# A chunked RWKV-7 scan: ScalarE copies the keys out of each score bank before VectorE masks it, and the stacked keys are copied later in the half-step

## The chip, the cores and the metric

The kernel runs on one core of one Trainium2 chip. The metric is the device time of one execution in microseconds. The core's engines run side by side, each through its own list of instructions in order: TensorE (PE in the profile; PEld is its weight load), VectorE (DVE), ScalarE (ACT), GpSimd (POOL, which here also issues DMAs) and SyncE (SP, which only issues DMAs). An instruction that needs another engine's result waits on a semaphore, and everything behind it on its own engine waits with it.

## The reference, cut to what matters

The model is a trunk of two layers over 1024 latent and 256 context tokens, width 1024, all in float32. Layer 0 mixes by pooling and neighbourhood attention, layer 1 by a bidirectional RWKV-7 recurrence, and each layer ends in an MLP. The change touches the recurrence of layer 1 alone. For each of 16 heads (64 wide) and each of two directions it is

```python
def step(S, inp):
    w_t, k_t, v_t, kk_t, kka_t = inp[:5]
    S = (S * w_t[:, :, None, :]
         - jnp.einsum('bhij,bhj->bhi', S, kk_t)[..., None] * kka_t[:, :, None, :]
         + v_t[..., None] * k_t[:, :, None, :])
    y = jnp.einsum('bhij,bhj->bhi', S, inp[5]) if emit else None
    return S, y
...
for d, reverse in enumerate((False, True)):
    decay_c, k_dc, a_c = dirs_c[d]
    s_ctx, y_c = wkv_scan(s0, decay_c, k_dc, v_c, kk_c, a_c, r_c, reverse)
    decay, k_d, a = dirs[d]
    _, y_d = wkv_scan(s_ctx, decay, k_d, v, kk, a, r, reverse)
    ys.append(y_d)
```

The context tokens come first and give the state from which the latent tokens start; only the latent tokens emit an output.

## The kernel before, in words

The scan (`l1_scan`, called once, after the features of layer 1) runs in chunks of 64 tokens: 20 steps `s`, of which 0 to 3 are context and 4 to 19 latent (`w["lat"]`). A step holds two half-steps, one for each direction `d`. All instructions of the loop stand in the order in which the code is written (a manual schedule); nothing reorders them.

In a half-step (s, d), three kinds of work are woven together.

- **The chain** of (s, d): `chain_x` multiplies the scores `ZQ[..., 1]` with the stacked state and values `D` into PSUM (`xp`), and ScalarE copies that to `XS` (L1679). `chain_u` multiplies by the chunk's inverse `TT` (`up`), and ScalarE writes the negative into `D` (L1688). `readout_state` (`yp`, L1701) and `readout_values` (`yp`, L1713) make the output, which ScalarE copies to `yt` (L1717) and SyncE stores. `chain_s` (`sp`, L1729) makes the new state, which VectorE adds and decays in two instructions (`SS`, L1734 and L1738). `carry`, called in the next half-step right behind `chain_x`, copies that state into the next step's `D` (two instructions, L1748) and then calls `stack`, which copies a part of the features `FT` into the upper half of the next step's `ZQ` (two instructions, L1608).
- **The scores** of the next step (n = s + 1, d): four groups `g`, two head pairs each. PE writes a group into the two PSUM banks of a tile `sc`, of which there are three. From these banks VectorE masks the scores into `ZQ` (L1632 for latent, L1639 for context steps) and ScalarE copies the token-major keys into `TM` (L1644).
- **The background**: `fill()`, called eight times in a half-step, takes the next pieces of the triangular inversions (`scan_invert`: two VectorE instructions each, L1511 and L1515), and from step 13 on pieces of the readout (`readout_sums`, L1966 to L1986, with long VectorE and GpSimd instructions over 128x1024) and splits of output weights.

For d = 1, `compose1` and `compose2` also run: two small products for the next inverse, with ScalarE's copies `G` (L1658) and `TT` (L1671). The pool `chps` gives the chain's products two PSUM buffers in turn, so a product waits until ScalarE or VectorE has emptied the one before the last.

A mask and a key copy of one group read the same two banks, and the program orders them by a semaphore: the key copy, second in the code, waits for the mask.

Of the kernel before, what the change touches and what calls it, by code (L numbers as in the profile page):

```python
# [58 lines left out]
class Trunk:  # L59
# [1466 lines left out]
    def l1_scan(self):  # L1526
        nc, a = self.nc, self.a
        with ExitStack() as es:
# [35 lines left out]
            def load(s, d, parts=range(4)):  # L1564

                if s >= NSTEP:
                    return
                w = W[s]
                F = w["F"][d] = FTs[(2 * s + d) % 4]
                f0 = 0 if w["lat"] else 1  # L1570
                for i in parts:
                    w["got"].add((d, i))
                    hs = slice(2 * i, 2 * i + 2)
                    (nc.scalar if s == 0 else nc.gpsimd).dma_start(out=F[:, hs, 1 + f0:], in_=self.ft[s, d, :, hs, f0:])

            def load_values(s, d):
                D_ = hp_.tile([128, 8, 2, CH], F32, tag=f"D{d}", name="D")
                (nc.gpsimd if s == 0 else nc.sync).dma_start(
                    out=D_[64:128], in_=rows_of(self.v1scr, s, d).rearrange("t (h e i) -> t h e i", e=2, i=CH)
                )  # L1580
                W[s]["D"][d] = D_
# [15 lines left out]
            def load_inverses(s, e):  # L1597
                if s >= NSTEP:
                    return
                TT = W[s]["TT"] = TTs[s % 2]  # L1600
                for bl in range(2):
                    r = slice(e * 64 + bl * 32, e * 64 + bl * 32 + 32)
                    nc.sync.dma_start(out=dh(TT[r, :, :, bl * 32:bl * 32 + 32]), in_=quarter(lt_[s // 2], s, bl, e))

            def stack(s, d):

                for e in range(2):
                    nc.scalar.copy(out=W[s]["ZQ"][d][0:64, :, e, 1], in_=W[s]["F"][d][st[e], :, 2])  # L1608

            def scores(s, d, g):  # L1610


                w = W[s]
                F = w["F"][d]
                more = s + 1 < NSTEP
                if g == 0:
                    w["ZQ"][d] = zp.tile([128, 8, 2, 2, CH], F32, tag="ZQ", name="ZQ")
                    if more:
                        w["TM"][d] = zp.tile([128, 8, 128], F32, tag="TM", name="TM")
                assert (d, g) in w["got"]  # L1620
                ps = scps.tile([128, 2, 512], F32, tag="sc", name="sc")
                p4 = ps[:, :, 0:384].rearrange("p e (j f t) -> p j e f t", j=2, f=3)
                f = slice(0, 3) if w["lat"] and more else slice(1, 3) if w["lat"] else slice(0, 3, 2)
                for j in range(2):
                    for e in range(2):
                        nc.tensor.matmul(
                            out=p4[:, j, e, f], lhsT=F[st[e], 2 * g + j, 3:5].rearrange("p a t -> p (a t)"), rhs=F[st[e], 2 * g + j, f],
                            start=True, stop=True,
                        )
                hs = slice(2 * g, 2 * g + 2)  # L1630
                if w["lat"]:
                    nc.vector.tensor_tensor(  # L1632
                        out=w["ZQ"][d][:, hs].rearrange("p j e f t -> p j e (f t)"),
                        in0=ps[:, :, 0:384].rearrange("p e (j n) -> p j e n", j=2)[:, :, :, CH:],
                        in1=masks[:, d, 1:3].rearrange("p f t -> p (f t)").unsqueeze(1).unsqueeze(1).to_broadcast([128, 2, 2, 2 * CH]),
                        op=ALU.mult,
                    )
                else:
                    nc.vector.tensor_tensor(  # L1639
                        out=w["ZQ"][d][64:128, hs, :, 1], in0=p4[64:128, :, :, 2],  # L1640
                        in1=masks[64:128, d, 2:3].unsqueeze(1).to_broadcast([64, 2, 2, CH]), op=ALU.mult,
                    )
                if more:
                    nc.scalar.copy(out=w["TM"][d][:, hs].rearrange("p j (e i) -> p j e i", e=2), in_=p4[:, :, :, 0])  # L1644

            def compose1(s):

# [25 lines left out]
            def chain_x(s, d):  # L1673
                w = W[s]
                xp = chps.tile([128, 8, CH], F32, tag="ch", name="xp")
                for h in range(8):
                    for e in range(2):
                        nc.tensor.matmul(out=xp[st[e], h], lhsT=w["ZQ"][d][:, h, e, 1], rhs=w["D"][d][:, h, e], start=True, stop=True)
                nc.scalar.copy(out=XSs[d], in_=xp)  # L1679
# [63 lines left out]
            def carry():  # L1743

                while late:
                    s, d = late.pop()
                    for e in range(2):
                        nc.scalar.copy(out=W[s]["D"][d][0:64, :, e], in_=SS[d][st[e]])  # L1748
                    stack(s, d)

            def background():

                blocks = self.scan_blocks(ip, NCC // 2, nc.sync.dma_start)
                for b in range(NCC // 2, NSTEP // 2):
                    yield
                    for i, _ in enumerate(self.scan_invert(ip, b, *blocks)):
                        if i == 16 and b + 1 < NSTEP // 2:
                            blocks = self.scan_blocks(ip, b + 1, nc.sync.dma_start)
                        yield
                pace[0] = 1  # L1760
                self.readout_weight_load(8)
                self.readout_weight_load(0)
                for _ in range(6):
                    yield
                self.readout_weight(8)
                yield
                self.readout_weight(0)
                yield
                self.readout_gate_load(READ_ORDER[0])
                yield from self.readout_all(READ_ORDER[:4], lambda t: step[0] >= EARLY[t])  # L1770
                self.readout_gate(READ_ORDER[0])
                self.readout_gate_load(READ_ORDER[1])
                for k in (1, 2, 3):
                    self.readout_weight_load(k)
                for _ in range(4):
                    yield
                self.readout_weight(1)
                self.readout_weight_load(4)

            bg, late = background(), []  # L1780

            pace, step, turn = [2.1], [0], [0]

            def fill():
                turn[0] += pace[0] / 2
                while turn[0] >= 1:
                    turn[0] -= 1
                    next(bg, None)
# [23 lines left out]
            for s in range(NSTEP - 1):  # L1812
                n = s + 1
                step[0] = s
                if s == 2:
                    pace[0] = 2.45
                later = ((s + 1, 1), (s + 2, 0)) if s else ((NSTEP, 1), (s + 2, 0))
                for d in range(2):
                    load_values(n, d)
                    chain_x(s, d)  # L1820
                    carry()
                    scores(n, d, 0)
                    load(*later[d], (2,))
                    fill()
                    scores(n, d, 1)
                    fill()
                    chain_u(s, d)
                    load(*later[d], (3,))
                    fill()
                    if d:  # L1830
                        compose1(n)
                    else:
                        load_blocks(s + 2, 0)
                    scores(n, d, 2)
                    fill()
                    readout_state(s, d)
                    chain_s(s, d)
                    load(s + 2, d, (0,))
                    fill()
                    readout_values(s, d)  # L1840
                    if d:
                        load_inverses(s + 2, 0)
                    else:
                        load_blocks(s + 2, 1)
                    fill()
                    scores(n, d, 3)
                    load(s + 2, d, (1,))
                    fill()
                    if d:
                        compose2(n)  # L1850
                        load_inverses(s + 2, 1)
                    fill()
            for _ in bg:
                pass
            s = NSTEP - 1
            for d in range(2):
                chain_x(s, d)
                carry()
            self.readout_weight(2)
            self.readout_weight_load(5)  # L1860
            for d in range(2):
# [384 lines left out]
```

## Time and profile before

| what | value |
| --- | --- |
| median of 3 runs | 3560.07 us (3559.86 to 3560.34) |
| the profiled execution | 3557.76 us, span 3555.6 us |
| mean granted TensorE clock | 0.962 |
| busy share of the span: PE, PEld, DVE, ACT, POOL | 93%, 77%, 58%, 40%, 12% |
| first and last product of `xp` (the scan) | 2208.6 and 2673.2 us |
| start of `XS` of step 3 d = 0, step 4 d = 0, step 18 d = 0 | 2281.47, 2303.00, 2646.55 us |
| duration of mask L1632, key copy L1644, stack copy L1608 | 684, 368, 617 ns (means) |

All times in the profile count from the start of the span. "Idle before" is the time for which an engine stood still before an instruction, with the instruction that released it. An engine's busy share over the whole span says little about the scan; there, one reads for each engine what its waits were and who ended them.

### The profile page before, as it was taken

The numbers are of one execution on the slowest core, as the hardware profiler recorded it, in microseconds if no ns is written. First come the engines' busy times: TensorE is split into PE (matmuls) and PEld (weight loads), VectorE is DVE, ScalarE is ACT, GpSimd is POOL, SyncE is SP. The second block draws the span as 40 slices with busy tenths as digits, with TensorE's granted clock in tenths as the row PEclk, the third lists the DMA queues.
The fourth block names the chain that finished last, engine by engine and source line by source line (L and its number), as shares of the span: only waits on it lengthen the run. The fifth ranks groups of instructions, "written<-read, shape, count | busy, mean of one in ns | idle before, by whom it ended". The sixth has DMA issues, their size and how long they took to land. (4 is left out here: it accounts for less than half of the span.)

```text
span 3555.6 us, 62546 instructions
## 1 busy us (share of the span) xinstructions
PE 3295.9 (93%) x25466; PEld 2752.1 (77%) x25466; DVE 2052.2 (58%) x3903; ACT 1434.7 (40%) x2743; POOL 430.9 (12%) x564
## 2 busy tenths in 40 slices
PE   8999889999999999989988776888888899999998
PEld 4787767888888888868878775777776788888887
DVE  4255555344444444596658997888665734444446
ACT  4244446311121211276667664556654521111112
POOL 0010110010000000024420002223241200000000
PEclk9999989999999999999999997899989999999999
DMA  8432333222222211143227678788763411111112
GB/s 280 151 91 83 102 126 132 88 84 83 83 84 83 76 44 36 42 148 100 70 69 222 211 232 243 159 196 202 214 177 116 165 49 48 48 48 48 48 48 77
DMA packets 432623, 409.11 MB, mean 115 GB/s; under 512 B 151584, under 2 KB 362400, under 8 KB 432336
## 3 DMA queue, kind: packets, MB, share of 16 engines
q1 hardware_dynamic: 405376, 321.55, 30.5%
q0 software_dynamic: 24640, 81.81, 7.4%
q8 instruction: 200, 3.28, 0.4%
q10 hardware_dynamic: 2320, 1.77, 0.2%
q14 instruction: 87, 0.71, 0.1%
HBM read 292.54 MB, written 112.49 MB: 114 GB/s over the span
## 5 line engine op out<-in xcount | busy, mean ns | idle before, releaser
L916 DVE TENSOR_TENSOR yacc<-yps,yacc 128x512 f32<-128x512 f32 x540 | 369.6, 689 | 304.3 <-PE yps L93 303.9
L74 ACT CAST wh<-st 128x1024 fp32r<-128x1024 f32 x160 | 165.0, 1049 | 760.5 <-PE yps L93 557.8
L93 PE MATMUL yps<-wh,xh 128*128 128x512 f32 x1152 | 453.3, 393 | 3.7 <-DVE yacc L916 2.1
L93 PE MATMUL yps<-wh,xl 128*128 128x512 f32 x1152 | 448.6, 390 | 0.7 <-DVE xl L75 0.7
L93 PE MATMUL yps<-wl,xh 128*128 128x512 f32 x1152 | 449.0, 390 | 0.0
L75 DVE TENSOR_TENSOR wl<-st,wh 128x1024 fp32r<-128x1024 f32 x160 | 194.2, 1228 | 277.6 <-ACT wh L74 277.5
L93 PE MATMUL acc<-h2h,wh 128*128 128x426 f32 (+3 forms) x768 | 275.7, 359 | 3.0 <-ACT y L671 3.0
L93 PE MATMUL acc<-h2h,wl 128*128 128x426 f32 (+3 forms) x768 | 274.2, 357 | 0.0
L93 PE MATMUL acc<-h2l,wh 128*128 128x426 f32 (+3 forms) x768 | 274.0, 357 | 0.0
L93 PEld LDWEIGHTS yps<-wh,xh 128*128 128x128 f32 x1152 | 216.2, 188 | 71.7 <-DVE yacc L916 12.7
L93 PEld LDWEIGHTS yps<-wh,xl 128*128 128x128 f32 x1152 | 216.2, 188 | 47.8 <-DVE xl L75 2.3
L93 PEld LDWEIGHTS yps<-wl,xh 128*128 128x128 f32 x1152 | 216.3, 188 | 44.9 <-issue 1.7
L898 DVE TENSOR_TENSOR r<-r 128x428 f32<-128x428 f32 (+4 forms) x164 | 102.3, 624 | 242.4 <-ACT r L897 242.4
L93 PE MATMUL acc<-mh,wh 128*128 128x256 f32 (+1 forms) x640 | 216.4, 339 | 4.3 <-ACT mh L74 4.2
L93 PE MATMUL acc<-ml,wh 128*128 128x256 f32 (+1 forms) x640 | 215.7, 337 | 0.0
L93 PE MATMUL acc<-mh,wl 128*128 128x256 f32 (+1 forms) x640 | 215.3, 337 | 0.0
L93 PE MATMUL acc<-h2bh,wh 128*128 128x512 f32 (+3 forms) x544 | 211.4, 389 | 1.4 <-ACT wh L74 0.7
L93 PE MATMUL acc<-h2bl,wh 128*128 128x512 f32 (+3 forms) x544 | 211.2, 388 | 0.7 <-DVE h2bl L288 0.7
L93 PE MATMUL acc<-h2bh,wl 128*128 128x512 f32 (+3 forms) x544 | 210.9, 388 | 0.3 <-DVE wl L75 0.3
L897 ACT ACTIVATE r<-acc 128x428 f32<-128x428 f32 (+4 forms) x164 | 89.1, 543 | 293.8 <-PE acc L93 269.0
L93 PEld LDWEIGHTS acc<-h2h,wh 128*128 128x128 f32 x768 | 145.0, 189 | 16.1 <-issue 5.1
L74 ACT CAST xh<-r 128x428 fp32r<-128x428 f32 (+4 forms) x164 | 93.3, 569 | 148.0 <-DVE r L898 148.0
(322 smaller groups left out, 7057.5 us busy)
## 6 DMA issues: line engine op xcount, KB each, us to landing
st<-in_mlp_w SPq DMA_DIRECT2D x128, 512.0 KB
ft<-F SPq DMA_DIRECT2D x64, 512.0 KB
FT<-ft POOLq DMA_DIRECT2D x128, 256.0 KB, 5.6
adas<-in_ada_w POOLq DMA_DIRECT2D x112, 256.0 KB, 3.8
adas<-in_ada_w SPq DMA_DIRECT2D x80, 256.0 KB
x<-x SPq DMA_DIRECT2D x28, 512.0 KB
bias<-in_bias SPq DMA_DIRECT2D x64, 192.0 KB
ls<-ls SPq DMA_DIRECT2D x80, 128.0 KB
```

Of the source, the lines that this page charges most:

```text
L74: self.nc.scalar.copy(out=hi, in_=src)
L75: self.nc.vector.tensor_tensor(out=lo, in0=src, in1=hi.bitcast(F32), op=ALU.subtract)
L93: self.nc.tensor.matmul(out=ps, lhsT=lhs[x], rhs=rhs[y], start=first and i == 0, stop=last and i == 2)
L897: nc.scalar.activation(out=r, in_=ps, func=AF.Relu)
L898: nc.vector.tensor_tensor(out=r, in0=r, in1=r, op=ALU.mult)
L916: nc.vector.tensor_tensor(out=yacc[t][:, n], in0=ps, in1=yacc[t][:, n], op=ALU.add)
```

## The change

It moves two things in each engine's list and takes nothing away. In `scores` the key copy is written ahead of the mask, so that the mask now waits for the key copy. In `carry` the call of `stack` is replaced by a note in the list `stacks`, which the loop works off behind the third group of scores; in the last step it is worked off right behind `carry`, as before.

```diff
                 hs = slice(2 * g, 2 * g + 2)
+                if more:
+                    nc.scalar.copy(out=w["TM"][d][:, hs].rearrange("p j (e i) -> p j e i", e=2), in_=p4[:, :, :, 0])
                 if w["lat"]:
                     nc.vector.tensor_tensor(
...
-                if more:
-                    nc.scalar.copy(out=w["TM"][d][:, hs].rearrange("p j (e i) -> p j e i", e=2), in_=p4[:, :, :, 0])
...
                     for e in range(2):
                         nc.scalar.copy(out=W[s]["D"][d][0:64, :, e], in_=SS[d][st[e]])
-                    stack(s, d)
+                    stacks.append((s, d))
...
-            bg, late = background(), []
+            bg, late, stacks = background(), [], []
...
                     scores(n, d, 2)
+                    while stacks:
+                        stack(*stacks.pop())
                     fill()
                     readout_state(s, d)
...
             for d in range(2):
                 chain_x(s, d)
                 carry()
+                while stacks:
+                    stack(*stacks.pop())
```

ScalarE in the half-step s = 8, d = 1, from the state's copy to the inverse's. Before, the stack copy (`ZQ`) stands between the state's copies (`D<-SS`) and the first key copies (`TM`), ahead of the chain's values (`D<-up`):

```order
L1679 COPY XS_19567<-xp 128x512
L1748 COPY D<-SS 64x8x64 x2
L1608 COPY ZQ<-FT_19564 64x8x64 x2
L1644 COPY TM<-sc 128x256 x2
L1688 ACTIVATE D<-up 64x8x64 x2
L1658 ACTIVATE G<-p_23001 32x512 x2
L1644 COPY TM<-sc 128x256
L1717 COPY yt<-yp 128x512
L1644 COPY TM<-sc 128x256
L1671 COPY TT_19569<-p_23125 32x16x32 x2
```

The same place now (line numbers are those of the changed file, in which the key copy is L1632):

```order
L1679 COPY XS_19567<-xp 128x512
L1748 COPY D<-SS 64x8x64 x2
L1632 COPY TM<-sc 128x256 x2
L1688 ACTIVATE D<-up 64x8x64 x2
L1658 ACTIVATE G<-p_22999 32x512 x2
L1632 COPY TM<-sc 128x256
L1608 COPY ZQ<-FT_19564 64x8x64 x2
L1717 COPY yt<-yp 128x512
L1632 COPY TM<-sc 128x256
L1671 COPY TT_19569<-p_23125 32x16x32 x2
```

The two stack copies moved behind the third key copy, just ahead of `yt`; no other instruction of ScalarE changed its place.

VectorE around the last mask ahead of the state update of the same half-step, with the semaphores that each row waits for (PE, DVE itself, Activation for ScalarE). Before:

```order
L1632 TENSOR_TENSOR ZQ<-sc,masks 128x512 [waits PE_49]
L1511 TENSOR_TENSOR tmp<-X,M 128x135 [waits DVE_49]
L1515 TENSOR_TENSOR X<-X,tmp 128x5x27 [waits DVE_49]
L1734 TENSOR_TENSOR SS<-sp,SS 128x512 [waits PE_49,Activation_49]
L1738 TENSOR_TENSOR SS<-SS,pcs 128x512 [waits DVE_49]
```

And now:

```order
L1634 TENSOR_TENSOR ZQ<-sc,masks 128x512 [waits Activation_49]
L1511 TENSOR_TENSOR tmp<-X,M 128x135 [waits DVE_49]
L1515 TENSOR_TENSOR X<-X,tmp 128x5x27 [waits DVE_49]
L1734 TENSOR_TENSOR SS<-sp,SS 128x512 [waits PE_49]
L1738 TENSOR_TENSOR SS<-SS,pcs 128x512 [waits DVE_49]
```

VectorE's order is the same; the mask waits for ScalarE instead of PE, and the key copies of ScalarE, which waited for VectorE before, now wait for PE alone. The lists of PE, POOL and SP keep their order; `chain_x`'s first products of `xp` now also wait for the stack copy, which is later.

## The prediction

> **What bounds the scan now.** I cut the scan into three stretches by the starts of `XS` and read busy time and granted clock in each. Columns: PE, PEld, VectorE, ScalarE and GpSimd busy, granted clock, DMA share, GB/s. The first row is context steps 1 to 3, the second steps 4 to 12 (full scores with inversions), the third steps 13 to 18 (inversions over, output weights and readout beside the scan).
>
> ```profile
> 2236.73:2303.00 66.27, 52.78 (x1168) 46.42 (x1164) 57.11 (x148) 39.01 (x78) 19.42 (x26) 0.87 0.74 163
> 2303.00:2516.17 213.17, 182.41 (x4608) 161.42 (x4608) 184.23 (x455) 127.89 (x253) 65.03 (x92) 0.97 0.81 196
> 2516.17:2668.46 152.29, 128.75 (x3060) 114.54 (x3056) 96.18 (x124) 92.15 (x173) 59.51 (x54) 0.89 0.72 197
> ```
>
> No engine is full. ScalarE works 60% of the time (127.89 of 213.17). So I asked who waits for whom, over the whole scan (us in total, times, longest):
>
> ```profile
> ACT TM L1644 <- DVE ZQ L1632: 86.2, 49, 6.1
> DVE SS L1734 <- PE sp L1729: 44.1, 30, 4.2
> ACT TM L1644 <- DVE ZQ L1639: 34.9, 13, 6.8
> PE sp L1729 <- ACT D L1688: 29.3, 24, 6.4
> PE yp L1701 <- ACT D L1688: 18.8, 14, 2.7
> PE up L1686 <- ACT XS L1679: 18.2, 19, 4.3
> ```
>
> A ring: ScalarE's key copy waits for a mask (86.2 + 34.9 = 121.1 us); behind it stand `XS` and the chain's values, for which PE waits (66.3 us); VectorE then waits for PE's `sp` (44.1 us). Masks stand behind inversions and readout on VectorE, so VectorE's backlog reaches PE through ScalarE.
>
> One half-step in order of time (step 8, d = 1), ScalarE first, then PE, then VectorE; the brackets hold the idle time before:
>
> ```profile
> 2409.24 0.37 ACT L1644 COPY TM<-sc 128x256 f32<-128x256 f32 x1 [1.56 <-DVE ZQ L1632]
> 2409.51 0.59 ACT L1679 COPY XS<-xp 128x512 f32<-128x512 f32 x1
> 2410.13 1.26 ACT L1748 COPY D<-SS 64x512 f32<-64x512 f32 x2
> 2411.41 1.25 ACT L1608 COPY ZQ<-FT 64x512 f32<-64x512 f32 x2
> 2412.57 0.63 ACT L1644 COPY TM<-sc 128x256 f32<-128x256 f32 x2
> 2413.09 1.21 ACT L1688 ACTIVATE D<-up 64x512 f32<-64x512 f32 x2
> 2414.33 1.19 ACT L1658 ACTIVATE G<-p 32x512 f32<-32x512 f32 x2
> 2415.54 0.37 ACT L1644 COPY TM<-sc 128x256 f32<-128x256 f32 x1
> 2417.70 0.58 ACT L1717 COPY yt<-yp 128x512 f32<-128x512 f32 x1 [1.79 <-PE yp L1713]
> ```
>
> ```profile
> 2408.91 1.57 PE L1626 MATMUL sc<-FT 64*128 64x192 f32 x16
> 2410.42 1.15 PE L1686 MATMUL up<-XS,TT 64*64 64x64 f32 x32
> 2411.49 1.20 PE L1653 MATMUL p<-ZT,G 32*32 32x32 f32 x64
> 2412.62 0.92 PE L1626 MATMUL sc<-FT 64*128 64x192 f32 x8
> 2414.36 1.15 PE L1701 MATMUL yp<-SS,FT 64*64 64x64 f32 x32 [0.81 <-ACT D L1688]
> 2415.57 1.15 PE L1729 MATMUL sp<-D,TM 128*64 128x64 f32 x32
> ```
>
> ```profile
> 2410.90 0.68 DVE L1632 TENSOR_TENSOR ZQ<-sc,masks 128x512 f32<-128x512 f32 x1
> 2413.59 0.69 DVE L1632 TENSOR_TENSOR ZQ<-sc,masks 128x512 f32<-128x512 f32 x1
> 2416.84 0.69 DVE L1734 TENSOR_TENSOR SS<-sp,SS 128x512 f32<-128x512 f32 x1 [2.01 <-PE sp L1729]
> ```
>
> `XS` is late because of the key copy; the values (2413.09) are late because 1.25 us of stack copies stand ahead of them; `yp` needs a PSUM buffer that the values empty, and waits 0.81.
>
> **The stack copies.** Moved, not removed: 74 of the 80 leave the place ahead of the values (the first step's four and two of the last stay). In the half-step above, `XS` would start right behind `xp` (about 2409.0), state copies end at 2410.9, two key copies at 2411.5, and the values wait for `up`, which ends at 2411.55: they run to 2412.8 instead of 2414.3. PE is through with `sc` at 2413.5 and starts `yp` there, not at 2414.36. In the new place the copies end at 2412.8 + 1.19 (`G`) + 0.37 + 1.25 = 2415.6. Next is `yt`, and the 1.79 us that ScalarE idled before it are the cover: `yp` would be complete at about 2416.7. If a readout piece filled that gap, `yt` would be late by up to 1.25, and with it the PSUM buffer. The copies also wait for the fourth mask of the half-step before; PE's third score group needs that mask's banks too (three tiles), so the wait is already over. `xp`, the reader, comes after 2418: nothing. No DMA moves; GpSimd's loads into `FT` a step later see the stack copy done, and SyncE's store of `yt` keeps its place.
>
> **The swapped pair.** ScalarE's copy then waits for PE only; the 121.1 us go, and what ScalarE gains lies idle unless PE gets `XS` and the values earlier. VectorE's mask pays: it starts no sooner than the key copy's end. The first mask, 2410.90 before, would wait to about 2411.2; the third needs its key copy, behind `G`, and moves from 2413.59 to about 2414.35. `SS` stands one mask and an inversion piece further on, at about 2415.85; `sp` ends at about 2415.7. So `SS` starts 1.0 us earlier than 2416.84, and VectorE, no longer PE, sets it. Next late are the state copy behind `SS` and PE's scores waiting for a mask's banks.
>
> **Steps 4 to 12.** The cap is what VectorE waits now, because its 455 instructions stay:
>
> ```profile
> DVE SS L1734 <- PE sp L1729: 18.0, 16, 3.1
> DVE ZQ L1632 <- PE sc L1626: 1.6, 3, 1.1
> ```
>
> 19.6 us; the half-step worked out gives 1.0, and eighteen of them 18. Where inversion pieces are short, PE sets the pace and some waiting stays; I take 14. Ends: 4, if the masks' new waits eat most of it, and 19.6.
>
> **Steps 0 to 3.** The same question from 2218 on, behind a wait for a DMA that stays:
>
> ```profile
> DVE SS L1734 <- PE sp L1729: 3.6, 3, 1.7
> DVE ZQ L1639 <- PE sc L1626: 1.8, 3, 1.4
> DVE SS L1738 <- PE sp L1729: 1.6, 2, 1.4
> ```
>
> 7.0 us at most; I take 4, near the share of the stretch above (14 of 19.6 would be 5), less a little because context scores are short and the key copies stand closer to the masks. Ends: -1 and 7.
>
> **Steps 13 to 18.** VectorE has room (96.18 of 152.29), but long readout instructions stand ahead of masks. Step 15, d = 1 (ScalarE, PE, VectorE):
>
> ```profile
> 2581.93 0.37 ACT L1644 COPY TM<-sc 128x256 f32<-128x256 f32 x1 [2.41 <-DVE ZQ L1632]
> 2582.20 1.21 ACT L1688 ACTIVATE D<-up 64x512 f32<-64x512 f32 x2
> ```
>
> ```profile
> 2579.83 0.92 PE L1626 MATMUL sc<-FT 64*128 64x192 f32 x8
> 2583.46 1.98 PE L1701 MATMUL yp<-SS,FT 64*64 64x64 f32 x32 [2.71 <-ACT D L1688]
> ```
>
> ```profile
> 2583.46 0.68 DVE L1632 TENSOR_TENSOR ZQ<-sc,masks 128x512 f32<-128x512 f32 x1
> 2587.38 0.69 DVE L1734 TENSOR_TENSOR SS<-sp,SS 128x512 f32<-128x512 f32 x1 [3.24 <-PE sp L1729]
> ```
>
> Here a key copy blocks the values until 2582.20. Free of it they follow `up` at about 2578.8 and end at 2580.0; `yp` then starts behind `sc`, at 2580.7, and `sp` ends near 2583. `SS` would come right behind the mask that ends at 2584.14: 3.2 us earlier. Such a half-step comes once in each of three readout steps: 3 x 3.2 = 9.6. The other nine I price at 0.9 each, a little under the 1.0 above: 8.1. Together 17.7, taken as 18. Ends: 8, if GpSimd and VectorE's long instructions are what counts, and 37, all PE idle time (152.29 - 128.75 = 23.5) with the clock it lost (11% of 128.75 = 14).
>
> Sum: 4 + 14 + 18 = 36 us off the profiled execution's 3557.76, which lies 2.3 below the median of the runs: 3560.07 - 36 = 3524. All lowest ends together give 11 us, all highest 64.
>
> Part of that 14 rests on the clock. Behind an idle time of 0.81 us `yp` took 1.15 us; behind 2.71 us it took 1.98. [...]
>
> **Rivals.**
>
> The wait changes sides but not its size: VectorE, with 184.23 of 213.17 us busy the fullest beside PE, stands at masks behind ScalarE's queue, and little comes back at `SS`. For it: a mask's copy is now third or fourth in a queue that holds the state copies (1.26) and `G` (1.19). Against it: in the half-step above the masks move by 0.3 and 0.76 and `SS` has 2.01 to give. Price: 4 for steps 4 to 12, 8 to 11 later, 1 in context: about 15 us off, 3545.
>
> Slower: the first mask of each half-step waits behind `XS` and the state copies (0.59 + 1.26 + 0.37 = 2.2 us from the end of `xp`), while its scores are there after 0.8. That is up to 1.4 us each in the 26 half-steps of steps 0 to 12: 36 us, against 26.6 us of VectorE waiting (19.6 + 7.0) that can absorb it. It decides from about 1.0 us a half-step on. With 1.4 everywhere and nothing gained later: +10 us, 3570. Against it: VectorE is usually late at the first mask, as at 2410.90. [...]
>
> No change: PE's waits for ScalarE give way to waits for `FT` loads or stored inverses. The DMA share is 0.81 in steps 4 to 12 and would rise to 0.81 x 213 / 199 = 0.87; no wait of PE for a load stands among the large ones above. Price: 0, 3560.
>
> Much more: all the idle time of PE closes, 50 us or more off, 3507.
>
> **How the numbers follow.** Forecast case 0.70 (3508 to 3536 by itself, two thirds of the way to its ends), much more 0.08, changed sides 0.14, no change 0.04, slower 0.04. A range of 3502 to 3547 holds the forecast case, most of the much-more case and most of the changed-sides case. 0.2% of 3560 is 7 us, about what this measurement can tell from no change: faster 0.92, same 0.04, slower 0.04.
>
> **What would show it.** Right: key copies no longer wait for masks; `XS` and the values stop being what PE waits for; in steps 4 to 12 VectorE's waits for `sp` are under 6 us and the stretch takes about 199 us; steps 13 to 18 take about 134; `D<-SS` waits for `SS` here and there. Wrong: large new rows in which masks wait for key copies, or `xp` for the stack copy, or `yt` late with PE waiting for it; or GpSimd's loads arriving behind the scores that need them.

## The result, and the profile after

The changed kernel takes 3536.67 us (median of four runs, 3529.58 to 3543.92); before took 3559.97 (four runs, 3554.97 to 3560.34). The ratio is 0.9938, 95% interval 0.9915 to 0.996: faster by 23 us, where 36 were forecast (3524, range 3502 to 3547). The profiled execution of after is the fastest, 3529.58 us, 28.2 under the profiled one of before.

The waits over the whole scan of after (us in total, times, longest; the key copy is now L1632, the mask L1634, in context steps L1641):

```profile
DVE ZQ L1634 <- ACT TM L1632: 43.7, 29, 6.2
DVE ZQ L1641 <- ACT TM L1632: 15.2, 8, 6.3
ACT XS L1679 <- PE xp L1678: 32.4, 26, 4.8
ACT TM L1632 <- PE sc L1626: 20.1, 42, 1.8
DVE SS L1734 <- PE sp L1729: 8.5, 11, 1.6
ACT D L1748 <- DVE SS L1738: 9.3, 4, 5.0
PE xp L1678 <- issue: 7.7, 4, 4.0
PE p L1667 <- issue: 7.6, 6, 2.4
```

The ring is open: no key copy waits for a mask (121.1 us before), VectorE's wait for `sp` fell from 44.1 to 8.5 us, and PE's waits for `XS` and the values (66.3 us) are gone from the head of the list. PE's waits for the stack copy ahead of `xp` did not grow (2.7 us, 2.6 before). Two things stand in their place: masks wait for key copies (58.9 us), and PE waits for "issue", that is for nothing the profile names.

The three stretches of after (same columns as before's three rows):

```profile
2230.83:2291.55 60.72, 50.50 (x1154) 44.63 (x1153) 55.91 (x144) 39.74 (x79) 19.34 (x26) 0.86 0.82 171
2291.55:2502.42 210.87, 185.38 (x4610) 164.60 (x4612) 186.00 (x462) 131.16 (x253) 66.08 (x93) 0.95 0.84 202
2502.42:2639.13 136.71, 124.54 (x3072) 110.97 (x3070) 94.32 (x127) 93.18 (x173) 58.32 (x54) 0.93 0.78 219
```

Against 66.27, 213.17 and 152.29: steps 1 to 3 lost 5.5 us (with step 0, which went from 26.76 to 23.39, it is 8.9), steps 13 to 18 lost 15.6, and the longest stretch, steps 4 to 12, only 2.3. (Another 2.5 us lie ahead of the first `XS`.) So the question is where the gain of steps 4 to 12 went.

The half-step worked out in the prediction (step 8, d = 1) came as worked out. PE, then VectorE:

```profile
2398.69 1.57 PE L1626 MATMUL sc<-FT 64*128 64x192 f32 x16
2403.25 1.15 PE L1701 MATMUL yp<-SS,FT 64*64 64x64 f32 x32
2404.33 1.15 PE L1729 MATMUL sp<-D,TM 128*64 128x64 f32 x32
```

```profile
2404.33 0.69 DVE L1634 TENSOR_TENSOR ZQ<-sc,masks 128x512 f32<-128x512 f32 x1 [0.51 <-ACT TM L1632]
2405.53 0.69 DVE L1734 TENSOR_TENSOR SS<-sp,SS 128x512 f32<-128x512 f32 x1
```

From the start of `sc` to `SS` it is 6.84 us, before 7.93: 1.09 earlier, where 1.0 was forecast. `yp` has no wait (0.81 before), the third mask pays 0.51.

Other half-steps of the stretch look different. PE's order of time in step 7 of after:

```profile
2375.83 1.02 PE L1701 MATMUL yp<-SS,FT 64*64 64x64 f32 x26
2379.70 0.39 PE L1701 MATMUL yp<-SS,FT 64*64 64x64 f32 x6 [2.84 <-issue]
...
2386.22 0.63 PE L1667 MATMUL p<-TT,G 32*32 32x32 f32 x15 [2.36 <-issue]
2386.78 1.98 PE L1678 MATMUL xp<-D,ZQ 128*64 128x64 f32 x32
2388.68 2.93 PE L1626 MATMUL sc<-FT 64*128 64x192 f32 x16
```

A run of 32 matmuls that needs nothing further stops for 2.84 us after the 26th; 127 matmuls later it happens again, and behind that pause `xp` takes 1.98 us instead of 1.15 and `sc` 2.93 instead of 1.57. Counted along PE's queue, such pauses of the stretch lie 127, 253, 378 to 379, 504 to 506 or 757 matmuls apart: multiples of about 126 (the expectations below write 128). The DMA queues of the stretch say why that number (packets, MB, share of 16 engines):

```profile
q8 instruction: 37, 0.61, 1.4%
```

37 packets for 4610 matmuls and 4612 weight loads are about 250 instructions each: PE's own instructions come by DMA, some 126 matmuls a packet. The trace has the time of every packet, and it shows that the pauses are blocks that come late: at each of the 13 pauses on these multiples (over 0.3 us) PE goes on 1.28 to 1.68 us after a packet of q8 has landed, and over all the kernels below, at 123 such pauses, 1.2 to 2.0 us after. The packet that ends the pause of 2.84 us, for one, starts to move at 2376.78 and lands at 2378.02. The pauses add up to 15.8 us in steps 4 to 12 of after, and to 2.3 us in before. Two more waits for "issue" in after, 1.81 and 1.63 us ahead of `xp`, lie off the multiples and follow no packet in this way; they are not counted, nor are their like below.

### The profile page after: what moved, and what is told of

The parts are those of the page before. It is cut to its first block, busy times and chain, and to the rows that moved or that the text cites. A ratio compares the mean times of both kernels' runs of the same rounds, so it can differ in the third digit from the quotient of the medians.

```text
span 3527.5 us, 62517 instructions
## 1 busy us (share of the span) xinstructions
PE 3289.8 (93%) x25466; PEld 2747.2 (78%) x25466; DVE 2049.0 (58%) x3903; ACT 1440.4 (41%) x2743; POOL 430.9 (12%) x564
## 5 line engine op out<-in xcount | busy, mean ns | idle before, releaser
L1626 PE MATMUL sc<-FT 64*128 64x192 f32 (+1 forms) x1280 | 144.3, 357 | 16.6 <-issue 6.5
```

The source lines that it names most:

```text
L1626: nc.tensor.matmul(out=p4[:, j, e, f], lhsT=F[st[e], 2 * g + j, 3:5].rearrange("p a t -> p (a t)"), rhs=F[st[e], 2 * g + j, f], start=True ...
```

## The experiments

All ratios are to the kernel before, timed on the same chip.

**Each part alone, and the change again.** `swap_only` keeps the key copy first and puts the stack copies back:

```
 carry():  -  stacks.append((s, d))
           +  stack(s, d)
```

> The swapped pair alone; the stack copies stay behind the state copies. Both theories: most of the gain is here, 15 to 20 us off before (about 3542), since the 121 us in which key copies waited for masks go; in steps 4 to 12 the values are still late by the 1.25 us of stack copies, so PE waits there for values again, about 8 us. Theory A (VectorE's backlog sets steps 4 to 12): that stretch is 209 to 213 us, as with the whole change. Theory B (PE's instructions come late, in blocks of 128 matmuls, when DMA is busy): pauses in the middle of PE's runs are fewer than the 14 us of the whole change, since PE waits elsewhere meanwhile.

`stack_only` moves the stack copies and keeps the mask first:

```
-                if more:
-                    nc.scalar.copy(out=w["TM"]...)     # ahead of the masks
...
+                if more:
+                    nc.scalar.copy(out=w["TM"]...)     # behind them
```

> The stack copies moved, the mask still ahead of the key copy. Key copies still wait for masks (over 90 us in all). Values come up to 1.25 us earlier where no key copy holds them up: 3 to 8 us off before (about 3555). No change at all would mean that the move alone is worth nothing without the swap.

`after_again` has no edit.

> The changed kernel a second time, for its spread. Theory A: the waits follow from the order of the program, so steps 4 to 12 take 210 to 212 us again and the pauses at blocks of 128 matmuls do not move the time. Theory B: the pauses differ from one execution to the next (they hang on what DMA is doing at that moment), and the stretch and the whole time move with their sum, about 1 us for each us of pause; runs spread over 10 us or more, while before stays within 6.

The swap alone: 3549.12 us against 3557.15, ratio 0.9974 (0.9964 to 0.9983). The stack copies alone: 3546.12, ratio 0.9968 (0.9955 to 0.9981). Both: 3530.87, ratio 0.9922 (0.991 to 0.9934). So 8.0 and 11.0 us apart, 26.3 together: neither part carries the change. The 7 us above the sum of the two are just clear of the spread of these runs; against the 23 us of the first result they would be 4. I had expected 15 to 20 of the swap and 3 to 8 of the stack copies. Steps 4 to 12 of each, in that order (length, PE, PEld, VectorE, ScalarE, GpSimd, clock, DMA share, GB/s):

```profile
2296.93:2513.65 216.72, 187.27 (x4610) 166.14 (x4610) 184.67 (x459) 129.04 (x253) 65.01 (x92) 0.93 0.80 194
```

```profile
2300.04:2506.04 206.00, 179.72 (x4594) 158.91 (x4596) 183.64 (x456) 128.99 (x252) 65.82 (x92) 0.98 0.82 202
```

```profile
2292.00:2506.43 214.43, 189.06 (x4610) 168.04 (x4612) 185.21 (x460) 131.35 (x252) 65.95 (x93) 0.93 0.83 197
```

The change again gives 214.43, 3.6 more than in the first profile and 1.3 more than before: in these steps no gain in length is shown at all. Seven of its pauses stand at the same matmuls of the queue as in the first profile (863, 990, 1874, 2001, 2506, 3389, 3895); all add up to 16.3 us. Each part alone has 4 us of them. The expectations on time missed here, of both theories: 214.43 and, with the swap alone, 216.72 lie above A's 210 to 212 and 209 to 213, and the five runs of the change spread over 7.7 us where B had 10 or more, those of before over 11.5 where B had 6.

**Lighter DMA, on both kernels.** From the third step on the stored inverses are not loaded:

```
-                for bl in range(2):
+                for bl in range(2 if s < 2 else 0):
```

> The changed kernel without the loads of stored inverses from the third step on (left out, the scan uses the old ones): about 16000 packets of 128 B less in steps 4 to 12, nothing else. Theory A: no instruction of VectorE, ScalarE or PE changes, so steps 4 to 12 stay at 211 us and the whole at the changed kernel's time, within 2 us. Theory B: the DMA share falls from 0.84 to about 0.74, the pauses of 14 us at blocks of 128 matmuls fall by half or more, steps 4 to 12 take 201 to 206 us and the whole is 8 to 15 us under the changed kernel.

> The kernel before, without the loads of stored inverses from the third step on. Theory P: before has 2 us of pauses in steps 4 to 12, since PE waits there for ScalarE and its instructions catch up meanwhile; lighter DMA is worth 0 to 4 us. If it is worth 8 us as in the changed kernel, then lighter DMA helps in some other way, and the pauses do not tell why the gain in steps 4 to 12 was small.

On the changed kernel: 3522.48 us (3520.01 to 3526.83), ratio 0.9903 (0.989 to 0.9916); 8.4 under the changed kernel by medians of the same chip, though the intervals overlap a little (0.991 to 0.9916). The pauses fall to 9.7 us, and the DMA share to 0.76:

```profile
2288.27:2492.30 204.03, 180.52 (x4610) 160.13 (x4610) 185.19 (x461) 130.96 (x252) 66.13 (x93) 0.97 0.76 199
```

On the kernel before: ratio 0.9994 (0.9984 to 1.0004), no change shown; its steps 4 to 12 take 212.61 us with 2.4 us of pauses. Theory B's times held on both, though the pauses fell by 40%, not by half. But the profile bears B out only in part: of the 6.8 us by which the stretch is shorter than in the first profile of the change (10.4 against the second), 2.0 are PE's idle time, since its waits for the sum into `SS` rose from 3.5 to 6.7 us; the rest is a higher clock. From here on A is called V (VectorE), B is called P (PE's packets).

**Is VectorE the bound? Its work taken away.** The inversions work on one row of each block:

```
-            m, n = c + 1, 31 - c
+            m, n = 1, 31 - c
```

> The changed kernel with the inversions' multiplications and subtractions cut to one row (the rest of each block is left out; as many instructions, each short): VectorE has 70 to 80 us less to do in steps 4 to 12 and is never late. Theory V: masks wait for PE only, PE's waits for the sum into SS go, and the stretch falls below 200 us, to what PE works (185) and a few us of values. Theory P: pauses of 14 to 16 us or more stay, and the stretch does not fall under 200 us.

The whole takes 3504.2 us, ratio 0.9852 (0.9838 to 0.9865), but about 20 of these 27 to 32 us lie ahead of the scan, where inversions run too (its first `XS` comes at 2189.35 instead of 2207 to 2210). From there to the first `XS` of step 19 it takes 433.2 us, the change 431.7 and 433.9. In steps 4 to 12:

```profile
2269.45:2479.52 210.07, 185.04 (x4610) 164.44 (x4610) 130.58 (x464) 131.11 (x252) 65.01 (x92) 0.95 0.86 200
```

```profile
DVE ZQ L1634 <- ACT TM L1632: 53.2, 33, 5.8
DVE SS L1734 <- PE sp L1729: 15.2, 13, 4.9
```

VectorE has 55 us less to do (70 to 80 were expected) and waits them away (68.4 us in these two rows); the stretch is as long as with all its work. The pauses grow to 23.0 us of the 25.0 in which PE is idle. This is the clearest run of the study: theory V, on which both my cap and the rival of the sides rested, is wrong, at least with DMA as it is here.

**Both left out**, lighter DMA and short inversions:

> The changed kernel with both left out: most of the inversions' work and the loads of stored inverses from the third step on. Theory V fell with the short inversions alone (steps 4 to 12 still took 210 us, with 23 us of pauses at blocks of 128 matmuls). Theory P (PE's instructions arrive too slowly while DMA is busy; what other waits give up, the pauses take): with less DMA and no late VectorE the pauses fall to about 10 us and nothing else takes their place, so steps 4 to 12 take 188 to 198 us. Theory C (PE's idle time of about 25 us is the chain xp, XS, up, values, yp of each half-step, and the pauses only show where PE would wait anyway): the stretch stays at 202 us or more.

```profile
2270.39:2469.13 198.74, 183.04 (x4610) 163.25 (x4612) 128.74 (x459) 130.88 (x253) 65.01 (x92) 0.96 0.77 197
```

198.74 us, just above what P gave and under what C gave; 3488.61 in all, ratio 0.9807 (0.9786 to 0.9829). PE's idle time (length less busy) goes to 15.7 us, all but 0.2 of it pauses, more than the 10 I expected. Theory C, a chain that leaves 25 us idle whatever ends it, does not fit. Nor is VectorE's work free everywhere: with the lighter DMA alone PE's idle time is 23.5 us, so here, where the pauses are shorter, the short inversions are worth 7.8 us of it.

**Three edits after theory V.** `hybrid` puts the mask first again in steps 4 to 12 alone (`scores` is called with the next step as its `s`):

```
+                first = more and not 5 <= s <= 13
```

> The changed kernel with the mask first again in steps 4 to 12 alone, the stack copies late everywhere, the key copy first in the other steps. Theory V (in steps 4 to 12 VectorE is what bounds, so what a mask waits for a key copy is lost, and the swap is worth nothing or less there): that stretch takes about 206 us, as with the stack copies moved alone, the other steps stay as in the changed kernel, and the whole is 5 to 8 us under it (about 3524). Theory P (PE's pauses at blocks of 128 matmuls took the gain of those steps, whichever copy is first): the stretch stays at 209 to 214 us and the whole within 3 us of the changed kernel.

3534.7 us, ratio 0.9938 (0.9925 to 0.9951): no better than the change itself, and the stretch did not come down to 206. V's numbers failed; P's were near (214 at most for the stretch), but not for P's reason: the pauses are 4.1 us, and the lower clock makes the stretch long. As a whole it is ahead of the stack copies alone (0.9968, 0.9955 to 0.9981), so the swap pays in the other steps; that it pays in steps 4 to 12 is not shown.

```profile
2293.63:2508.35 214.72, 188.06 (x4624) 167.06 (x4624) 186.30 (x462) 129.46 (x252) 65.85 (x92) 0.94 0.80 197
```

`carry_late` and `ss_early`:

```
 carry_late                      ss_early
-  carry()                       -  fill()
   scores(n, d, 0)                  readout_state(s, d)
+  carry()                          chain_s(s, d)
                                 +  fill()
```

> The changed kernel with the state copies (1.26 us in each half-step) behind the first key copy instead of ahead of it, so that the first mask waits for XS alone. Theory V: mask waits in steps 4 to 12 fall from 13 to 16 us to under 9, the stretch from 211-214 to 204-208 us, and the whole comes 5 to 10 us under the changed kernel. Theory P: mask waits fall, but the stretch stays above 209 us since the pauses stay.

> The changed kernel with one piece of inversion moved from ahead of the sum into SS to behind it: VectorE reads sp, and so gives back PE's buffer, some 0.7 us earlier in about half of the half-steps. Theory V: PE's waits for the sum (3.5 us named, and as much unnamed ahead of xp) go, but VectorE now waits for sp; from nothing to 5 us off the changed kernel. Theory P: no change beyond 2 us.

`carry_late`: 3537.34 us, ratio 0.9943 (0.993 to 0.9955), no gain. Masks wait 15.8 us in steps 4 to 12, not under 9, so the edit did not even do to the waits what both theories said. `ss_early`: 3527.28, ratio 0.9922 (0.9906 to 0.9937), as the change itself; PE's waits for the sum fall from 3.5 to 2.1 us and its pauses rise to 17.7.

**More DMA, and the same DMA in smaller bursts.** `more_dma` adds, in each half-step from step 4 on, two copies of 512 packets to a spare part of DRAM:

```
+                    if s > 3:
+                        extra(s, d)
```

> The changed kernel with two extra copies in each half-step from step 4 on, from one part of DRAM to a spare part that nobody reads, 512 packets of 128 B each: as many packets more as the loads of stored inverses were. Theory P: pauses in steps 4 to 12 go from 15 to over 20 us and the whole is 5 to 15 us over the changed kernel. Theory C: no engine waits for these copies; within 3 us of the changed kernel, unless waits for loads by name appear.

3532.8 us, ratio 0.9938 (0.9925 to 0.995). The DMA share rose to 0.89, the pauses to 17.4 only, the time not beyond its spread. P's 5 to 15 us did not come: the number of small packets alone did not lengthen the pauses beyond 17.4. `spread_blocks` issues the eight block loads of an inversion one by one:

```
-  if i == 16 and ...: blocks = self.scan_blocks(...)
+  if i >= 10 and i % 2 == 0 and ...: blocks = next(parts, None) or blocks
```

> The changed kernel, complete, with the eight loads of the inversions' next blocks (512 packets of 128 B each, issued together at the seventeenth piece of an inversion) issued one by one, at every second piece from the eleventh on; X is set up after the last. No load more or less, only less of a burst. Theory P with bursts (an instruction block comes late when all 16 DMA engines are busy for some us on end): the pauses in steps 4 to 12 fall from about 16 us to about 10, those near the old bursts most, and the whole is 3 to 8 us under the changed kernel, which would beat both. Theory P with the mean load (what counts is how many packets there are in all): pauses and time stay, within 3 us. Theory C (PE's idle time is the chain of each half-step): time stays as well, and if pauses do fall, waits for ScalarE or for the sum into SS take their place.

3526.87 us, ratio 0.9904 (0.9888 to 0.9919), steps 4 to 12 in 206.24 us:

```profile
2292.44:2498.68 206.24, 184.99 (x4610) 164.48 (x4612) 185.21 (x462) 131.53 (x252) 66.53 (x93) 0.95 0.87 204
```

The pauses fell to 14.2 us, not to 10. It is the fastest complete kernel run here and beats before; against the change (0.9922, 0.991 to 0.9934, and 0.9938) the intervals overlap, so that it beats the change is not shown.

**The account of steps 4 to 12.** Idle is length less PE busy; pauses are PE's waits for "issue" of over 0.3 us at block borders, the multiples above. One profile each, whole stretch:

| kernel | length | PE busy | clock | idle | pauses |
|---|---|---|---|---|---|
| before | 213.17 | 182.41 | 0.97 | 30.8 | 2.3 |
| before, lighter DMA | 212.61 | 183.02 | 0.96 | 29.6 | 2.4 |
| swap alone | 216.72 | 187.27 | 0.93 | 29.5 | 4.2 |
| stack copies alone | 206.00 | 179.72 | 0.98 | 26.3 | 4.1 |
| hybrid | 214.72 | 188.06 | 0.94 | 26.7 | 4.1 |
| changed | 210.87 | 185.38 | 0.95 | 25.5 | 15.8 |
| changed, again | 214.43 | 189.06 | 0.93 | 25.4 | 16.3 |
| changed, one piece behind `SS` | 213.84 | 189.31 | 0.93 | 24.5 | 17.7 |
| changed, state copies later | 217.69 | 189.92 | 0.92 | 27.8 | 17.1 |
| changed, more DMA | 213.16 | 188.22 | 0.94 | 24.9 | 17.4 |
| changed, blocks spread | 206.24 | 184.99 | 0.95 | 21.3 | 14.2 |
| changed, lighter DMA | 204.03 | 180.52 | 0.97 | 23.5 | 9.7 |
| changed, short inversions | 210.07 | 185.04 | 0.95 | 25.0 | 23.0 |
| changed, both | 198.74 | 183.04 | 0.96 | 15.7 | 15.5 |

Two columns tell it. Busy times clock is 174 to 177 us in every row: PE's work. What differs is the clock and the idle time, and idle stays at 24 to 31 us through all reorderings of the other engines; only what it consists of changes. It goes under 24 only where DMA is lighter or smoother, and only in the changed kernel (29.6 in the kernel before with lighter DMA). The clock is worth as much as the waits: hybrid and the stack copies alone have the same order of work in these steps and differ by 8.7 us, 8.3 of it in PE busy. So one profile of this stretch says no more than about 4 us either way, and no row alone is a verdict.

## Why the prediction was right, and where not

The mechanism came: the ring opened and the chain moved up. The time, 3536.67, lies inside the range, just beyond the 3508 to 3536 of the forecast case; those ends are worked out wrongly, for two thirds of the way to all lowest and all highest ends (11 and 64 us off) are 3541 and 3505. Two of the three terms were too high and one too low, and that the errors partly cancelled is luck.

**The half-step and the swapped pair.** Right in the mechanism: the queue order of ScalarE, `yp` without a wait, the third mask later, `SS` 1.09 us earlier. The working let both parts meet in one time for the values (2412.8 instead of 2414.3) and priced them only together; the runs bear this out: 8.0 and 11.0 apart, 26.3 together. "Masks waiting for key copies" stood among the signs that would show the forecast wrong. They came, 58.9 us of them, and in steps 4 to 12 they cost little, as the next point shows.

**Steps 4 to 12: 14 us taken, 2.3 measured, and -1.3 the second time.** This is the term that failed, outside its own ends of 4 and 19.6. The step that failed is the extrapolation from one half-step to eighteen under a cap of VectorE's waits. VectorE did give its waits for `sp` back (18.0 to 2.1 us, forecast under 6), and masks took 13.2 of them, so the rival of the sides describes the waits well. But short inversions show that VectorE does not set the time: without 55 us of its work the stretch is 210.07. PE sets it, and PE gained only 5.3 us of idle time (30.8 to 25.5), because 13.5 us of new pauses came where these 28.7 us of before went:

```profile
PE yp L1701 <- ACT D L1688: 11.2, 9, 2.0
PE up L1686 <- ACT XS L1679: 8.9, 12, 1.6
PE sp L1729 <- ACT D L1688: 8.6, 9, 1.1
```

The clock then took 3.0 us back (PE busy 182.41 to 185.38; 6.7 in the second profile). The rows for it stood in before: PE is busy 182.41 of 213.17, and beside it the DMA share of 0.81. I looked for a load that PE waits for and did not ask how PE's instructions come.

**Steps 0 to 3: 4 us taken, 8.9 measured (11.2 again).** Above its end of 7. Steps 1 to 3 gave 5.5 and 6.8, inside the cap; the cap began at 2218 and left out most of the first half-step, where PE in before waited longest of all for the values:

```profile
2220.69 2.59 PE L1729 MATMUL sp<-D,TM 128*64 128x64 f32 x32 [6.37 <-ACT D L1688]
```

The same wait is 0.29 us in after. Step 0 gave 3.4 and 4.4. The term was sized on the wrong stretch.

**Steps 13 to 18: 18 us taken, 15.6 measured (14.6 again).** Near. Here the pauses hardly grew, 5.9 us in after, 4.8 in before; idle fell from 23.5 to 12.2 us and the clock rose from 0.89 to 0.93, so PE busy fell by 4.2. That lost speed would come back with the gaps was right here.

**The clock.** The prediction set 1.98 us of `yp` behind an idle time of 2.71 us. After has the same slow matmuls behind shorter idle times still:

```profile
2470.21 0.32 PE L1626 MATMUL sc<-FT 64*128 64x192 f32 x1 [1.25 <-issue]
2470.46 1.96 PE L1701 MATMUL yp<-SS,FT 64*64 64x64 f32 x32
2472.35 1.85 PE L1729 MATMUL sp<-D,TM 128*64 128x64 f32 x32
2474.03 1.10 PE L1713 MATMUL yp<-D,ZQ 128*64 128x64 f32 x32
```

An idle time of 1.25 us is followed by 3.8 us at 1.7 times the duration, 1.5 us lost. The granted clock before, during and behind it (the columns of the stretches; a packet counts whole where it starts, so over 3.41 us the DMA share can pass 1):

```profile
2467.10:2470.51 3.41, 2.16 (x74) 1.58 (x68) 3.20 (x11) 2.37 (x4) 0.00 (x0) 1.00 1.11 176
2470.51:2473.93 3.42, 3.42 (x63) 3.30 (x64) 2.06 (x5) 1.61 (x3) 2.36 (x3) 0.50 0.90 245
2473.93:2477.34 3.41, 3.41 (x122) 3.08 (x120) 2.88 (x9) 1.14 (x3) 2.46 (x4) 1.00 1.00 316
```

The clock was halved for 3.41 us, behind 3.41 us in which PE had been busy for 2.16. The 2.84 us before (2379.70) is followed by no such fall; the next comes at 2385.18, in the second pause. In the scans of all 14 traces the granted clock is 1.00 or 0.50 and changes only at borders 3.41 us apart. Taken from 2210 us on, 125 such windows a trace, a window at full clock in which PE was busy for under 46% was always followed by half clock, one of over 74% never; between these both occur, and what decides there was not found. In before and after, with 211 windows at full clock, the busiest that half clock followed had 69%, the least busy that full clock followed 55%. The borders lie elsewhere in each trace (one at 2470.51 in after, one at 2319.35 in before, which is no whole number of windows away), and one order of work gave seven stretches at half clock in hybrid (24.8 us of steps 4 to 12) and two in the stack copies alone (10.2 us). The window ahead of the fall above was idle for only 1.25 of its 3.41 us.

**What stays open.** The pauses follow the change (both parts together, about 16 us), grow when nothing else stops PE (23.0) and shrink with lighter DMA (9.7). Why a packet is late is open. In after none of the 37 starts to move more than about one block ahead of the one that it brings, and ahead of the two pauses of over 2 us it starts only near the end of that block; once it moves it takes 0.9 to 2.1 us. Packets start late where DMA is full: over steps 4 to 12 of all 14 traces, the 114 that started within 1 us of PE's entering the block before had a DMA share of 0.66 in the first 3 us of that block, the 191 that started 2 to 4 us in had 0.94 to 0.97 (the 77 later still 0.84). That goes together; it does not show which is the cause. One view close up, after around the pause that ends at 2493.72 (40 slices of 0.25 us, from 2486; busy tenths of the 16 engines):

```profile
DMA  2799979998999999999999999992410000030000
```

The engines are full from 2486.5 to 2492.75, the packet moves from 2491.23 to 2492.30, and PE resumes at 2493.72. But 19 thousand more packets did not lengthen the pauses beyond 17.4, and spreading the block loads took off only 1 to 2 us. Which traffic holds up the packet was not settled.

## What to carry to other kernels

When one engine is near full, price a removed wait by what that engine does next, not by the waits of the engine that complains most; the test is to take the other engine's work away and see whether the time moves. Look in the trace for stops in the middle of a run of matmuls, count the matmuls between them, and compare with the instruction queue's packets, in number and in time: as long as such stops take up what the other waits give back, reordering other engines buys little (PE's idle time stayed at 24 to 31 us here). Two edits that shorten the same path may be worth more together than the sum of each alone (26.3 us against 8.0 and 11.0 here), so time them together before dropping one.

## What the runs showed of the hardware that was not expected

- PE's instructions arrive by DMA in packets of about 250 (in after, 37 packets for 9222 instructions in 211 us). PE stopped at block borders for up to 3.7 us (`ss_early`), in stretches whose DMA share was 0.76 to 0.89, and went on 1.2 to 2.0 us after a packet had landed.
- The clock was halved for 3.41 or 6.83 us at a time in these steps, behind windows of 3.41 us in which PE was busy for up to 73%; matmuls then took 1.7 times their duration (`yp` 1.96 us against 1.15). One and the same order of work had 10 us of half clock in one execution and 25 in another (stack copies alone and hybrid), and 200 us of it differed by 8 us in PE busy (179.72 and 188.06).
